# 27 chunks of u turned by VectorE beside the mixer instead of 24, from weight piece 10 on, and spread evenly

## The chip, the cores and the metric

One core of a Trainium2 chip runs the whole kernel. The metric is the time on the device in microseconds, the median over runs. A profile is one execution with the hardware profiler; its span is from the first to the last instruction.

TensorE (PE; its weight loads are PEld), VectorE (DVE), ScalarE (ACT) and GpSimd (POOL) each work through their own instructions in order. SP only issues transfers. Transfers issued by SP, by ScalarE and by POOL go through three queues to the same 16 transfer engines.

## The reference

A decoder layer over 256 tokens of width 1024: a mixer and then a product-key retrieval over 16384 experts (PEER), whose tables `u` and `v` have 16384 rows of 1024 floats each.

```python
h = rmsnorm(x)
proj = h @ w_in                       # 1024 x 6656
... retention, block attention with a relative-position bias, two branches, gates, w_out ...
x = x + merged @ w_out
h2 = rmsnorm(x)
# PEER: 8 heads, the 16 best of 128 x 128 experts for each token
u = u_tab[experts]
a = gelu(einsum('td,thkd->thk', h2, u))
x = x + einsum('thk,thkd->td', gates * a, v_tab[experts])
```

## The kernel before, in words

**The mixer** (to about 250 us) takes all its weights in 72 pieces of 256 rows by 512 columns (512 KB each), in the loop over `i`. SP loads a piece into a ring of six buffers (`raw_ring`, L206). ScalarE cuts off its high half (`rhi`, L151), VectorE the rest (`rlo`, L152), three pieces ahead of TensorE, which multiplies it in 12 matmuls (L234 to L236: high by high, low by high, high by low). Between the pieces `pump` advances the epilogues and the attention a step each. The attention adds the relative-position bias to its scores on VectorE (`pr<-side,bias`, L369), takes the maximum (`smx`, L373), and ScalarE the exponentials (L375). `bias` comes from 8 transfers of 128 KB out of a skewed table, issued by POOL (L840). POOL also has the small powers for the normalisations (`qky`, L158) and the sums of the rotary step (`ra`, L328).

**The dense stage** (about 300 to 635 us) multiplies all of `u`, in 128 chunks of 128 rows, with part of the tokens. A chunk `c` is loaded by SP into the same ring (L674), turned by 8 transposes on TensorE (L732) two chunks ahead, brought back from PSUM by ScalarE, and then multiplied (L1304; 8 products, which the trace counts as 16). In the same time POOL gathers single rows of `u` and `v`, VectorE forms dot products with them, and from about 465 us on one-hot matrices are multiplied in between (L1225, L1226). 14 chunks (`HELD`) are loaded ahead into another buffer and are not in the ring. The third stage (635 to 895 us) does the same with `v`, without transposes.

**The turned chunks** are the subject of the change. `EARLY` lists chunks that are turned during the mixer, one each at the weight pieces in `TURNED`. For the m-th, `early_turns` issues at piece `TURNED[m]` - 4 four transfers of 128 KB on POOL's queue (L742) into a buffer `raw`; at `TURNED[m]` and one piece later VectorE turns half of it each (L746) from `raw` to `dst`; another piece later ScalarE writes `dst` to the tensor `turned` in HBM (L770). In the dense stage SP loads such a chunk from `turned` (L697) and TensorE multiplies it without transposes. There are three buffers for `raw` and three for `dst`: `eraw` and `eT`; `h2` (named `h` in the trace) and a part of `hTf`; and as third first parts of `sa` and `ret`, later the two halves of the attention's tile `pr`.

The order on each engine is the order in which the code is written (`manual_schedule`), so a step that moves in the loop moves on every engine that it uses. Waits are put in where data or buffers need them. Each transfer of POOL's queue gets one of eight semaphores in turn (`DMASW0` to `DMASW7`) and is not issued before the last transfer with the same semaphore has landed.

Of the kernel before, what the change touches and what calls it, by code (L numbers as in the profile page):

```python
# [50 lines left out]
HELD = [0, 1, 2, 8, 14, 21] + list(range(26, 62, 6)) + [61, 66]  # L51
HELD0 = 2
FOLD = 104
TURNED = list(range(14, 36, 2)) + [37, 40, 42, 45, 48, 50, 53, 56, 58, 61, 64, 66, 69]
EARLY_RAW = [0, 1, 2, 0, 1, 2, 0, 1, 2, 0, 1, 0] + [2, 1, 0] * 4
EARLY_AT = [-3 if m == 11 else -4 for m in range(24)]
NPRE = len(TURNED)
EARLY = [3 + 5 * m + (m in (1, 7)) for m in range(NPRE)]
TURN = (124, 126)
TURN0 = 95  # L60
WARM = 8
# [18 lines left out]
def layer_kernel(ctx, tc, x, mix_norm_g, w_in, ret_w_branch, moba_q_gain, moba_k_gain, moba_w_branch,  # L80
# [26 lines left out]
    def raw_tile(n=1):  # L107

        i = raw_count[0] % RAWS
        raw_count[0] += n  # L110
        assert i + n <= RAWS
        return raw_ring[:, i] if n == 1 else raw_ring[:, i:i + n]
# [102 lines left out]
    def products(i):  # L215
# [30 lines left out]
        if k0 + 2 == kc:  # L246
# [11 lines left out]
    early = ([ap.tile([P, D], F32, name="eraw"), h2],  # L258
             [ap.tile([P, D], F32, name="eT"), hTf.rearrange("p k t -> p (k t)")[:, :D]])
# [421 lines left out]
    def load_any(i):  # L681
# [9 lines left out]
        elif i < len(pieces) + NK:  # L691
# [3 lines left out]
            if early_chunk(c):  # L695
                u_raw[c] = raw_tile()
                nc.sync.dma_start(u_raw[c], turned[EARLY.index(c)])  # L697
            else:
# [36 lines left out]
    def early_chunk(c):  # L735
        return c in EARLY

    def load_quarters(queue, dst, c, quarters=range(4)):

        src = peer_u[0, c * P:(c + 1) * P, :].rearrange("(b a) (g d) -> g a b d", a=32, g=4)  # L740
        for g in quarters:
            queue.dma_start(dst[32 * g:32 * g + 32].rearrange("a (b d) -> a b d", b=4), src[g])  # L742

    def turn(dst, src, k):

        V.transpose(dst.rearrange("p (k b a) -> p b k a", k=KC, b=4)[:, :, k],  # L746
                    src.rearrange("p (b k i) -> p b k i", b=4, k=KC)[:, :, k])

    free = []

    def early_buffers(m):

        raw, dst = EARLY_RAW[m], m % 3
        if m >= EARLY_RAW.index(2, 11) and not free:
            t = wk.tile([P, H, S], F32, name="pr").rearrange("p h k -> p (h k)")
            free.extend([t[:, :D], t[:, D:]])
        third = free or [sa[:, KC // 2:].rearrange("p k t -> p (k t)"), ret[:, 1]]
        return (*early[0], third[0])[raw], (*early[1], third[1])[dst]

    def early_turns(i):  # L760

        for m in range(NPRE):
            step = i - TURNED[m]
            if step == EARLY_AT[m]:
                load_quarters(nc.gpsimd, early_buffers(m)[0], EARLY[m])
            if step in (0, 1):
                raw, dst = early_buffers(m)
                turn(dst, raw, slice(4 * step, 4 * step + 4))
            elif step == 2:
                nc.scalar.dma_start(turned[m], early_buffers(m)[1])  # L770
# [30 lines left out]
    for t in range(NT):  # L801
        for q in range(2):
            c = slice(512 * q, 512 * (q + 1))
# [46 lines left out]
    for i in range(n_mixer + 3):  # L850
        load_to(i + 1)
        if i == 8:
            nc.sync.dma_start(decay, c_decay)
        if i == 12:
            nc.sync.dma_start(grow2, row(ffn_norm_g))
        cut(i + 3)
        products(i)
        early_turns(i)
        pump()
# [422 lines left out]
    for c in range(NK):  # L1282
# [11 lines left out]
        m, g = divmod(c - TURN0, 8)  # L1294
# [171 lines left out]
```

## Time and profile before

| | us |
|---|---|
| median of 3 runs (lowest to highest) | 933.49 (931.58 to 933.52) |
| the profiled execution | 930.01 |
| its span | 928.2 |

TensorE's clock was granted in full. Of the page, the first lines give each engine's busy time and share; the slices cut the span into 40 parts of 23.2 us with the busy share of each in tenths; the chain is followed back from the last instruction. In a timeline row stand the start, the length, the engine, line, operation, what it writes and reads, the shape, the count, and in brackets how long the engine stood idle before and what ended that.

### The profile page before, as it was taken

How to read it: one execution, taken by the hardware profiler on the slowest of the kernel's cores; microseconds unless marked ns; L12 is line 12 of the kernel's file. 1: busy time of each engine (PE TensorE's matmuls, PEld its weight loads, DVE VectorE, ACT ScalarE, POOL GpSimd, SP SyncE). 2: the span in 40 equal slices, each digit the busy share in tenths (PEclk: the TensorE clock that was granted, in tenths of full speed). 3: DMA queues.
4: the chain of work that ended last, by engine and by line, in shares of the span. 5: the costliest groups of instructions: out<-in, count | busy, mean ns of one | idle time of the engine just before them, and what ended most of it. 6: DMA issues, size and time to landing. Idle time of an engine off the chain costs nothing.

```text
span 928.2 us, 18735 instructions
## 1 busy us (share of the span) xinstructions
PE 921.4 (99%) x6968; PEld 875.5 (94%) x6968; DVE 801.7 (86%) x1535; ACT 510.2 (55%) x940; POOL 450.4 (49%) x411
## 2 busy tenths in 40 slices
PE   9999999999999999999999999999999999999998
PEld 6887888888999999999999999999999999999997
DVE  6658666888778999999899999886989989898996
ACT  5555655544644535434587777676454545454553
POOL 3547233220102447534557786664656656474530
PEclk9999999999999999999999999999999999999999
DMA  9899998999799999999999999999999999999991
GB/s 312 244 256 296 346 288 259 353 327 292 237 372 383 399 386 351 387 397 378 375 408 405 391 381 369 385 408 373 368 397 408 409 407 409 385 408 379 388 392 59
DMA packets 107018, 328.83 MB, mean 354 GB/s; under 512 B 12237, under 2 KB 16246, under 8 KB 106799
## 3 DMA queue, kind: packets, MB, share of 16 engines
q1 hardware_dynamic: 64092, 183.07, 54.2%
q0 software_dynamic: 37440, 128.52, 38.0%
q10 hardware_dynamic: 5394, 16.05, 4.5%
q8 instruction: 55, 0.90, 0.4%
q14 instruction: 37, 0.30, 0.1%
HBM read 311.78 MB, written 17.33 MB: 355 GB/s over the span
## 4 chain that ended last, share of the span: by engine, by line
PE 73%; DVE 0%; ACT 0%; issue 0%; DVEq 0%
PE acc L1304 25%; PE side L732 10%; PE acc L1336 10%; PE side L1336 9%; PE acc L1337 4%; PE side L1337 4%; PE side L1334 2%; PE acc L1334 2%; PE acc L244 1%; PE acc L243 1%; PE acc L245 1%; PE acc L1226 1%; PE acc L1225 1%; PE side L624 1%; PE side L890 0%; PE side L587 0%
## 5 line engine op out<-in xcount | busy, mean ns | idle before, releaser
L1044 POOL DMA_INDIRECT rows<-in_peer_u_dram,eg x86 | 109.5, 1273 | 77.9 <-DVE rows L1055 37.9
L1044 POOL DMA_INDIRECT rows<-in_peer_v_dram,eg x54 | 100.1, 1854 | 75.4 <-DVE vacc L1132 58.0
L732 PE MATMUL side<-ident,raw_ring 128*128 128x128 f32 x704 | 94.6, 277 | 0.2 <-DMA raw_ring<-in_peer_u_dram 0.2
L732 PEld LDWEIGHTS side<-ident,raw_ring 128*128 128x128 f32 x704 | 85.3, 192 | 0.3 <-issue 0.3
L1270 ACT ACTIVATE cw<-W 128x352 fp32r<-128x352 f32 x58 | 28.9, 498 | 73.7 <-PE acc L1337 73.7
L1175 ACT ACTIVATE oh_buf<-oh_more,tS 128x128 bf16<-128x128 f16 x176 | 58.7, 414 | 12.5 <-DVE oh_more L1170 8.7
L1055 DVE SCALAR_TENSOR_TENSOR rows<-rows,h 128x1024 f32<-128x1024 f32 x43 | 53.5, 1254 | 5.2 <-DMA rows<-in_peer_u_dram,eg 5.2
L1132 DVE SCALAR_TENSOR_TENSOR vacc<-rows,av,vacc 128x1024 f32<-128x1024 f32 x42 | 53.7, 1279 | 0.1
L1304 PE MATMUL acc<-hTd,raw_ring 128*128 128x128 f32 x384 | 46.8, 275 | 0.0
L1271 DVE TENSOR_TENSOR cw<-W,cw 128x352 fp32r<-128x352 f32 x58 | 30.2, 521 | 17.1 <-ACT cw L1270 16.8
L1304 PEld LDWEIGHTS acc<-hTd,raw_ring 128*128 128x128 f32 x384 | 44.8, 192 | 0.0
L1256 POOL TENSOR_TENSOR W<-W,gl 128x256 f32<-128x256 f32 (+19 forms) x31 | 25.6, 825 | 28.3 <-ACT gl L1255 23.4
L1171 DVE TENSOR_TENSOR oh_buf<-oh_more,tM 128x1024 f16<-128x1024 f16 x44 | 32.2, 732 | 2.2
L742 POOL DMA_DIRECT2D eraw<-in_peer_u_dram x36 | 19.8, 555 | 26.5 <-DVE pr L746 14.1
L1170 DVE TENSOR_TENSOR oh_more<-iota,tI 128x1024 f16<-128x1024 f16 x44 | 32.0, 728 | 0.0
L742 POOL DMA_DIRECT2D h<-in_peer_u_dram x32 | 17.4, 551 | 25.2 <-DVE hTf L746 22.6
L1225 PE MATMUL acc<-oh_buf 128*128 128x128 bf16 x176 | 24.4, 219 | 0.0
L1226 PE MATMUL acc<-oh_buf 128*128 128x128 bf16 x176 | 24.4, 219 | 0.0
L1239 ACT ACTIVATE W<-acc 128x512 f32<-128x512 f32 (+20 forms) x44 | 17.0, 387 | 6.6 <-PE acc L1226 4.4
L1258 ACT ACTIVATE W<-acc 128x256 f32<-128x256 f32 (+19 forms) x52 | 18.5, 355 | 3.3 <-PE acc L1304 3.3
L1225 PEld LDWEIGHTS <-oh_buf 128*128 128x128 f16 x176 | 19.8, 113 | 0.0
L1226 PEld LDWEIGHTS <-oh_buf 128*128 128x128 f16 x176 | 19.7, 114 | 0.0
(2685 smaller groups left out, 3412.9 us busy)
## 6 DMA issues: line engine op xcount, KB each, us to landing
raw_ring<-in_peer_v_dram SPq DMA_DIRECT2D x100, 512.0 KB
raw_ring<-in_peer_u_dram SPq DMA_DIRECT2D x88, 512.0 KB
raw_ring<-in_w_in_dram SPq DMA_DIRECT2D x52, 512.0 KB
W<-in_peer_v_dram SPq DMA_DIRECT2D x28, 512.0 KB
raw_ring<-turned SPq DMA_DIRECT2D x24, 512.0 KB
raw_ring<-in_peer_w_q_dram SPq DMA_DIRECT2D x16, 512.0 KB
W<-in_peer_u_dram SPq DMA_DIRECT2D x14, 512.0 KB
eraw<-in_peer_u_dram POOLq DMA_DIRECT2D x36, 128.0 KB
```

The lines of the kernel that those rows point to most:

```text
L732: T.transpose(p[:, k * P:(k + 1) * P], r.rearrange("p (i k) -> p k i", k=KC)[:, 4 * q + k], ident)
L742: queue.dma_start(dst[32 * g:32 * g + 32].rearrange("a (b d) -> a b d", b=4), src[g])
L1044: G.indirect_dma_start(out=r, out_offset=None, in_=tab, in_offset=bass.IndirectOffsetOnAxis(ap=eg[:, j:j + 1], axis=0))
L1055: V.scalar_tensor_tensor(r, r, 1.0, h, op0=OP.mult, op1=OP.mult, accum_out=av[:, j:j + 1])
L1132: V.scalar_tensor_tensor(a, r, av[:, j:j + 1], a, op0=OP.mult, op1=OP.add)
L1175: A.activation(o1[:, j], hot[:, 0, :, j], AF.Copy, scale=tS[:, t, k + j:k + j + 1])
L1225: T.matmul(p[:, j * P:(j + 1) * P], hi, o1, start=True, stop=False)
L1226: T.matmul(p[:, j * P:(j + 1) * P], lo, o1, start=False, stop=True)
L1304: T.matmul(pa[:, n:n + NA], uT[:, k * P:(k + 1) * P], hT[:, k], start=(c % 2 == 0 and k == 0), stop=(k == KC - 1), skip_group_check=True)
L1334: T.matmul(o[b][:, :ND], vh[:, n], w, start=False, stop=False, skip_group_check=True)
L1336: T.matmul(o[b][:, :2 * ND], vh[:, n], w, start=(c == 0), stop=False, skip_group_check=True)
L1337: T.matmul(o[b][:, :ND], vl[:, n], w[:, :ND], start=False, stop=(c == NK - 1), skip_group_check=True)
```

## The change

`TURNED` gets three more places: pieces 10 and 12 at the front, and one more between 37 and 70, where the distance is 2.5 pieces throughout. `EARLY`, which was every fifth chunk from 3 to 118, is now spread evenly over the chunks 3 to 120 that are not held: 3, 7, 12, 17, 22, 27, 31, 37, 42, 47, 52, 57, 62, 67, 71, 75, 79, 83, 87, 91, 96, 100, 104, 108, 112, 116, 120. The tables for the `raw` buffer and the time of the load are gone: every load is issued four pieces ahead, `raw` and `dst` both go by m modulo 3, and the halves of `pr` come in at m = 14 (piece 40).

```diff
-TURNED = list(range(14, 36, 2)) + [37, 40, 42, 45, 48, 50, 53, 56, 58, 61, 64, 66, 69]
-EARLY_RAW = [0, 1, 2, 0, 1, 2, 0, 1, 2, 0, 1, 0] + [2, 1, 0] * 4
-EARLY_AT = [-3 if m == 11 else -4 for m in range(24)]
+TURNED = list(range(10, 36, 2)) + [37, 40, 42, 45, 47, 50, 52, 55, 57, 60, 62, 65, 67, 70]
 NPRE = len(TURNED)
-EARLY = [3 + 5 * m + (m in (1, 7)) for m in range(NPRE)]
+LEAD = 4
+LATE = 14
+EARLY = [c for c in range(3, 121) if c not in HELD]
+EARLY = [EARLY[round(m * (len(EARLY) - 1) / (NPRE - 1))] for m in range(NPRE)]
...
-        raw, dst = EARLY_RAW[m], m % 3
-        if m >= EARLY_RAW.index(2, 11) and not free:
+        if m == LATE and not free:
...
-        return (*early[0], third[0])[raw], (*early[1], third[1])[dst]
+        return [(*early[i], third[i])[m % 3] for i in range(2)]
...
-            if step == EARLY_AT[m]:
+            if step == -LEAD:
```

Line numbers up to the turned chunks are one higher in the changed kernel. POOL's instructions from the skewed table on, before:

```order
L832 DMA skew<-rr 8x16x384
L158 TENSOR_TENSOR qky<-qkss,minus_half 128x16 x2
L840 DMA bias<-skew 16x8x256 x8
L742 DMA eraw<-in_peer_u_dram 32x4x256 x4
L742 DMA h_75<-in_peer_u_dram 32x4x256 x4
L742 DMA sa<-in_peer_u_dram 32x4x256 x4
L328 TENSOR_TENSOR ra<-ra,rb__621 128x512
```

And now:

```order
L832 DMA skew<-rr 8x16x384
L159 TENSOR_TENSOR qky<-qkss,minus_half 128x16
L743 DMA eraw<-in_peer_u_dram 32x4x256 x4
L159 TENSOR_TENSOR qky<-qkss,minus_half 128x16
L743 DMA h_75<-in_peer_u_dram 32x4x256 x4
L840 DMA bias<-skew 16x8x256 x8
L743 DMA sa<-in_peer_u_dram 32x4x256 x4
L743 DMA eraw<-in_peer_u_dram 32x4x256 x4
L743 DMA h_75<-in_peer_u_dram 32x4x256 x4
L329 TENSOR_TENSOR ra<-ra,rb__635 128x512
```

The four loads of the first new chunk stand ahead of the second `qky`, and those of the second new chunk ahead of the eight transfers of `bias`. With the waits, the transfers of `bias` in the changed kernel are these:

```order
L743 DMA h_75<-in_peer_u_dram 32x4x256 [waits DMASW5_49]
L840 DMA bias<-skew 16x8x256 [waits DMASW6_49]
L840 DMA bias<-skew 16x8x256 [waits DMASW7_49]
L840 DMA bias<-skew 16x8x256 [waits DMASW0_49]
L840 DMA bias<-skew 16x8x256 [waits DMASW1_49]
L840 DMA bias<-skew 16x8x256 [waits DMASW2_49]
L840 DMA bias<-skew 16x8x256 [waits DMASW3_49]
L840 DMA bias<-skew 16x8x256 [waits DMASW4_49]
L840 DMA bias<-skew 16x8x256 [waits DMASW5_49]
```

Semaphores 6, 7, 0 and 1 were last given to the four loads of the first new chunk, 2 to 5 to those of the second. VectorE about pieces 14 to 17 of the weights (`rlo__493`, 532, 556 and 579), before:

```order
L152 TENSOR_TENSOR rlo__493<-raw_ring,rhi__492 128x1024
L369 TENSOR_TENSOR pr<-side,bias 128x4x128
L152 TENSOR_TENSOR rlo__532<-raw_ring,rhi__531 128x1024
L369 TENSOR_TENSOR pr<-side,bias 128x4x128
L152 TENSOR_TENSOR rlo__556<-raw_ring,rhi__555 128x1024
L373 TENSOR_REDUCE smx<-pr 128x8
L152 TENSOR_TENSOR rlo__579<-raw_ring,rhi__578 128x1024
```

And now (the same pieces are `rlo__502`, 542, 568 and 592):

```order
L747 STREAM_TRANSPOSE eT<-eraw 128x4x4x32
L153 TENSOR_TENSOR rlo__502<-raw_ring,rhi__501 128x1024
L747 STREAM_TRANSPOSE eT<-eraw 128x4x4x32
L370 TENSOR_TENSOR pr<-side,bias 128x4x128
L153 TENSOR_TENSOR rlo__542<-raw_ring,rhi__541 128x1024
L747 STREAM_TRANSPOSE hTf<-h_75 128x4x4x32
L370 TENSOR_TENSOR pr<-side,bias 128x4x128
L153 TENSOR_TENSOR rlo__568<-raw_ring,rhi__567 128x1024
L747 STREAM_TRANSPOSE hTf<-h_75 128x4x4x32
L374 TENSOR_REDUCE smx<-pr 128x8
L153 TENSOR_TENSOR rlo__592<-raw_ring,rhi__591 128x1024
```

Two transposes of the first new chunk stand ahead of `pr<-side,bias`, and the two of the second between it and `smx`. SP's loads in the last part of the dense stage, before:

```order
L697 DMA raw_ring<-turned 128x1024
L674 DMA raw_ring<-in_peer_u_dram 128x1024 x4
L697 DMA raw_ring<-turned 128x1024
L674 DMA raw_ring<-in_peer_u_dram 128x1024 x4
L697 DMA raw_ring<-turned 128x1024
```

And now:

```order
L698 DMA raw_ring<-turned 128x1024
L675 DMA raw_ring<-in_peer_u_dram 128x1024 x3
L698 DMA raw_ring<-turned 128x1024
L675 DMA raw_ring<-in_peer_u_dram 128x1024 x3
L698 DMA raw_ring<-turned 128x1024
```

From chunk 67 on three chunks, mostly, stand between two turned ones, where there were four.

## The prediction

> **What bounds the kernel now.** I read the engine line and the slices of the page first, then the chain of waits, then stretches of the timeline.
>
> ```profile
> PE 921.4 (99%) x6968; PEld 875.5 (94%) x6968; DVE 801.7 (86%) x1535; ACT 510.2 (55%) x940; POOL 450.4 (49%) x411
> PE   9999999999999999999999999999999999999998
> DMA  9899998999799999999999999999999999999991
> PE 73%; DVE 0%; ACT 0%; issue 0%; DVEq 0%
> ```
>
> TensorE is busy in every slice and the chain is TensorE's own work, so a microsecond taken off TensorE is a microsecond gained as long as nothing makes it wait, and one that it stands still is lost for good. But the transfer engines are as full as TensorE, so the margins by which data arrives ahead of it are the second thing to read.
>
> The gain lies in the stage over the 128 chunks of u. The chain of waits there, in order of time (start, duration, what):
>
> ```profile
> 483.40 0.95 PE side L732 x8
> 484.34 1.79 PE acc L1304 x16
> 486.58 0.95 PE side L732 x8
> 487.52 1.79 PE acc L1304 x16
> 489.31 0.89 PE side L732 x8
> 490.20 1.79 PE acc L1304 x16
> 492.43 1.84 PE acc L1304 x16
> 494.72 0.95 PE side L732 x8
> ```
>
> Each chunk has 8 transposes (L732) and its products (L1304); at 492.43 a turned chunk has products alone. From one chunk's transposes to the next takes 486.58 - 483.40 = 3.18 us, the turned one 494.72 - 492.43 = 2.29 us: 0.89 us less.
>
> The price lies in the mixer, where the early loads and the 8 transfers of `bias` share POOL's one queue. POOL's timeline there:
>
> ```profile
> 24.61 3.98 POOL L158 TENSOR_TENSOR qky<-qkss,minus_half 128x16 f32<-128x16 f32 x1 [3.05 <-DVE gain L834]
> 36.03 2.92 POOL L158 TENSOR_TENSOR qky<-qkss,minus_half 128x16 f32<-128x16 f32 x1 [7.44 <-DVE qkss L298]
> 38.90 4.27 POOL L840 DMA_DIRECT2D bias<-skew  x8
> 45.62 2.43 POOL L742 DMA_DIRECT2D eraw<-in_peer_u_dram  x4 [2.45 <-DMA bias<-skew]
> 52.31 0.55 POOL L742 DMA_DIRECT2D h<-in_peer_u_dram  x1 [0.46 <-DMA bias<-skew]
> 53.76 0.55 POOL L742 DMA_DIRECT2D sa<-in_peer_u_dram  x1 [0.90 <-DMA eraw<-in_peer_u_dram]
> 57.86 0.55 POOL L742 DMA_DIRECT2D sa<-in_peer_u_dram  x1 [0.60 <-DMA eraw<-in_peer_u_dram]
> ```
>
> A transfer on this queue waits until the one eight before it has landed (the order of the program shows it as one of eight semaphores). So these rows date landings: the first `bias` transfer is in by 45.62, the eighth by 52.31, the ninth (first of `eraw`) by 53.76 and the twelfth (last of `eraw`) by 57.86. Twelve transfers of 128 KB issued from 38.90 on take until 57.86, eight until 52.31.
>
> VectorE, in order, waits for all eight of `bias` before its next operation:
>
> ```profile
> 45.12 1.23 DVE L152 TENSOR_TENSOR rlo__493<-raw_ring,rhi__492 128x1024 fp32r<-128x1024 f32 x1 [2.50 <-ACT rhi__492 L151]
> 52.76 0.69 DVE L369 TENSOR_TENSOR pr<-side,bias 128x512 f32<-128x512 f32 x1 [6.41 <-DMA eraw<-in_peer_u_dram]
> 53.37 1.22 DVE L152 TENSOR_TENSOR rlo__532<-raw_ring,rhi__531 128x1024 fp32r<-128x1024 f32 x1
> 56.23 1.21 DVE L373 TENSOR_REDUCE smx<-pr 128x8 f32<-128x1024 f32 x1
> 60.12 1.23 DVE L152 TENSOR_TENSOR rlo__579<-raw_ring,rhi__578 128x1024 fp32r<-128x1024 f32 x1 [2.67 <-ACT rhi__578 L151]
> 65.01 0.70 DVE L746 STREAM_TRANSPOSE eT<-eraw 128x512 f32<-128x512 f32 x1
> 65.64 0.66 DVE L324 TENSOR_TENSOR ra<-acc,rope 128x512 f32<-128x512 f32 x1
> 66.98 1.17 DVE L152 TENSOR_TENSOR rlo__639<-raw_ring,rhi__638 128x1024 fp32r<-128x1024 f32 x1
> ```
>
> The wait of 6.41 us at 52.76 is put down to `eraw`, but L369 reads `bias`, and it ends 0.45 us after the eighth `bias` transfer is known to be in. Queued behind it are the low halves of the weights that TensorE multiplies (L152). When TensorE takes them:
>
> ```profile
> 56.17 0.39 PE L235 MATMUL acc<-rlo__532,hh 128*128 128x512 f32 x1
> 62.50 0.40 PE L235 MATMUL acc<-rlo__579,hh 128*128 128x512 f32 x1
> 68.39 0.40 PE L235 MATMUL acc<-rlo__639,hh 128*128 128x512 f32 x1
> ```
>
> Piece 15 (rlo__532) is ready at 53.37 + 1.22 = 54.59, 1.58 us ahead; piece 17 (rlo__579) at 61.35, 1.15 us ahead; piece 19 (rlo__639) at 68.15, 0.24 us ahead. These are the thinnest margins of the mixer after its first pieces, and they stand just where the two new chunks are put.
>
> **The change, part by part.**
>
> Three chunks fewer to transpose: 3 x 0.89 = -2.67 us (with 0.95 of the L732 rows instead, -2.85). ScalarE's 6 evacuations go too; ScalarE is 55% busy and is worth nothing here. All three lie late: 14 turned chunks up to chunk 68 before and after, 10 beyond it before, 13 now.
>
> The transfers of that stage. A turned chunk is read once like any other, so the bytes stay; they are asked for in less time. The rows of the stages and the one wait of TensorE in it:
>
> ```profile
> 450.00:550.00 100.00, 100.00 (x982) 100.00 (x981) 95.85 (x170) 76.51 (x218) 70.46 (x60) 1.00 1.02 398
> 550.00:600.00 50.00, 49.83 (x496) 49.67 (x494) 46.48 (x78) 37.56 (x109) 34.95 (x30) 1.00 1.03 375
> 600.00:635.00 35.00, 35.00 (x341) 35.00 (x340) 25.49 (x42) 23.80 (x61) 20.89 (x20) 1.00 1.03 404
> 596.28 1.14 PE L732 MATMUL side<-ident,raw_ring 128*128 128x128 f32 x8 [0.17 <-DMA raw_ring<-in_peer_u_dram]
> ```
>
> The columns after the length are busy PE, PEld, DVE, ACT and POOL, the clock, the share of the transfer engines and GB/s. At 596 TensorE already waits for a load, so around 570 to 605 (chunks 105 to 118) the margin is gone. Between chunks 95 and 118 one more chunk is turned than before (6 against 5), so TensorE asks 0.89 us sooner there and can wait up to that much. Between 0 and 0.89 I take +0.4, the middle. VectorE at 96% in 450:550 would be at 97% with 1% less time: no wait. [...]
>
> The two new early loads. Chunk 0's four transfers now follow the first `qky` (end 24.61 + 3.98 = 28.59), and POOL stands idle until 36.03, so they and VectorE's two transposes of 0.63 us (65.64 - 65.01) are hidden by VectorE's and POOL's own waits (VectorE stands 2.50 us before 45.12). Chunk 1's four come after the second `qky`, at 38.95, where `bias` stood, and `bias` follows them. `bias` then is the fifth to twelfth transfer of the burst, not the first to eighth. The twelfth landed by 57.86 and the eighth by 52.31: +5.55 us. The semaphore of the one eight before does not starve the queue: the last four of `bias` go out when chunk 1's have landed, as `eraw` did at 45.62.
>
> Two things move this. How the queues share the engines in that time (queue, packets, MB, share), first from 52.3 to 57.9, and then the write of one turned chunk, from 66 to 70:
>
> ```profile
> q0 software_dynamic: 321, 0.91, 72.1%
> q1 hardware_dynamic: 221, 0.42, 32.2%
> ...
> q10 hardware_dynamic: 144, 0.52, 32.4%
> ```
>
> With VectorE standing still SP runs out of free ring buffers, so less weight traffic (q1) competes: without any, 5.55 x 0.721 = 4.0 us is the lower bound. Against it, ScalarE now writes chunk 0 out at about 48 us, 0.52 MB that takes 32.4% of 4 us = 1.3 us: 6.85 us is the upper bound. They pull opposite ways and I stay at 5.55, the measured row. [...]
>
> What follows on VectorE: between L369 and the low half of piece 17 stand two more transposes (chunk 1's), 1.26 us, which lengthen the way L369, smx, ScalarE's exponentials, piece 17. So L152 of piece 15 comes 5.55 later (margin 1.58: TensorE waits 3.97), piece 17 comes 6.81 later (1.15: 5.66 in all) and piece 19 also 6.81 later (0.24): 6.57 us in all. Behind 70 us the chunks stand at the distances that they had, TensorE is as late as everything else, and the margins are as before: +6.57. Bounds: 4.0 + 1.02 = 5.0 and 6.85 + 1.02 = 7.9.
>
> The third new chunk stands at piece 70; its last transpose (0.63 us) falls before the last residual's chain. Between 0 and +0.63; before it VectorE idles about as long there, so 0. The buffers of the other chunks change places without a transfer being later than four pieces ahead: 0.
>
> **Sum.** +6.57 - 2.67 + 0.4 = +4.3 us on the profiled execution's 930.01 us. That one stands 3.5 us under the median of the runs, 933.49; the forecast is on the median: 937.8 us. What a measurement tells from no change is about 0.2%, 1.9 us.
>
> **Rivals.**
> 1. The queue moves faster than the rows say, and `bias` comes 0 to 3 us late: stall up to 4.1, net between -1.9 and +1.9, say 934.5. For it: the twelve would move with VectorE and SP silent. Against: even without all of q1 the rows give 4.0.
> 2. The end on the other side: `bias` is not held up. If the four of chunk 1 cost the queue under about 1.2 us, the stall (d + 1.02) is less than the 2.27 gained in the dense stage. Place: POOL's queue at 39 to 52 us; it decides at `bias` in by 53.5. With no delay at all but the two transposes, 1.26 - 0.24 = 1.0 is lost at piece 19, net -1.3; if that is hidden too -2.3: about 931.5. For it: the engines' queues run in parallel. Against: the ninth to twelfth landed one after another, 53.76 to 57.86.
> 3. The transfers of the dense stage eat the whole gain: +6.57 - 2.67 + 2.67 gives 940.1. For it: the wait at 596.28; against: 398 to 404 GB/s on both sides of it.
>
> **Chances.** The forecast with its own bounds, +2.2 (5.0 - 2.85) to +6.1 (7.9 - 2.67 + 0.89), 0.66; rival 3 and worse, 0.11; rival 1, 0.13; rival 2, 0.10. So slower 0.77, same 0.13, faster 0.10. Range: the forecast's own is 935.7 to 939.6; with rival 3 and half of rival 1 it is 934.0 to 941.0.
>
> **What would show it.** Right: `bias` issued from about 41 us on; L370 (`pr`) starting at 57 to 60 after an idle time of 10 us or more on VectorE; TensorE idle 3 to 5 us at about 56 and again at about 66; the mixer's end some 6 us later; in the dense stage 24 transposes fewer and the stage 2 to 3 us shorter. Wrong: L370 by 54 us, or a pause in TensorE's products that another engine makes up later, or a dense stage no shorter.

## The result, and the profile after

| | before | after |
|---|---|---|
| median of 5 runs each, taken together (lowest to highest), us | 933.23 (930.88 to 933.52) | 939.20 (937.92 to 940.66) |
| ratio, 95% interval | 1 | 1.0071 (1.0054 to 1.0089) |
| profiled execution, its span, us | 930.01, 928.2 | 938.77, 937.0 |

The change costs 0.71%, which is 5.0 to 8.3 us by the interval. Four lines of its page: busy time by engine, the slices of TensorE and of the transfer engines, and the chain of waits by engine.

```profile
PE 922.7 (98%) x6944; PEld 874.4 (93%) x6944; DVE 806.8 (86%) x1541; ACT 507.1 (54%) x934; POOL 454.7 (49%) x423
PE   8989999999999999999999999999999999999998
DMA  9999998999899999999999999999999999999991
PE 60%; DVE 23%; DMA 10%; POOL 2%; issue 2%; ACT 1%; SPq 0%; ACTq 0%; DVEq 0%; POOLq 0%
```

TensorE has 24 matmuls fewer and is busy 1.3 us longer; the third slice (47 to 70 us) is no longer full. The chain that was TensorE's alone now runs over VectorE for 23% and over transfers for 10%.

Where the 8.75 us of span are. POOL's timeline in the mixer after the change:

```profile
29.30 2.26 POOL L743 DMA_DIRECT2D eraw<-in_peer_u_dram  x4
36.78 2.93 POOL L159 TENSOR_TENSOR qky<-qkss,minus_half 128x16 f32<-128x16 f32 x1 [5.22 <-DVE qkss L299]
39.68 2.23 POOL L743 DMA_DIRECT2D h<-in_peer_u_dram  x4
41.90 2.11 POOL L840 DMA_DIRECT2D bias<-skew  x4
44.48 2.17 POOL L840 DMA_DIRECT2D bias<-skew  x4 [0.46 <-DMA h<-in_peer_u_dram]
...
58.80 0.55 POOL L743 DMA_DIRECT2D eraw<-in_peer_u_dram  x1 [0.45 <-DMA bias<-skew]
```

Chunk 1's loads (`h`) stand before `bias`. The issue at 58.80 waits for the eighth `bias` transfer (8 later on the queue), which therefore is in only then; before, it was at 52.31. VectorE's timeline, which waits for it:

```profile
45.87 1.23 DVE L153 TENSOR_TENSOR rlo__502<-raw_ring,rhi__501 128x1024 fp32r<-128x1024 f32 x1 [1.88 <-ACT rhi__501 L152]
...
58.83 0.69 DVE L370 TENSOR_TENSOR pr<-side,bias 128x512 f32<-128x512 f32 x1 [11.12 <-DMA sa<-in_peer_u_dram]
59.44 1.22 DVE L153 TENSOR_TENSOR rlo__542<-raw_ring,rhi__541 128x1024 fp32r<-128x1024 f32 x1
60.57 0.70 DVE L747 STREAM_TRANSPOSE hTf<-h 128x512 f32<-128x512 f32 x1
...
67.38 1.23 DVE L153 TENSOR_TENSOR rlo__592<-raw_ring,rhi__591 128x1024 fp32r<-128x1024 f32 x1 [2.67 <-ACT rhi__591 L152]
...
74.24 1.17 DVE L153 TENSOR_TENSOR rlo__653<-raw_ring,rhi__652 128x1024 fp32r<-128x1024 f32 x1
```

This execution was 0.75 us later than the one before from its start on (45.87 against 45.12). Apart from that, L370 starts 58.83 - 52.76 - 0.75 = 5.32 us later, and the low half of piece 19 (`rlo__653`, before 66.98) 6.51 us later. The stage borders of the kernel before, from TensorE's timeline (first product of chunk 0, first of the third stage):

```profile
299.05 1.17 PE L1304 MATMUL acc<-hTf,rhi__2891 128*128 128x128 f32 x9
638.69 0.41 PE L1336 MATMUL side<-cw,rhi__7232 128*128 128x352 f32 x1
```

And of the kernel after:

```profile
306.24 0.94 PE L1304 MATMUL acc<-hTf,rhi__2912 128*128 128x128 f32 x7
647.39 0.41 PE L1336 MATMUL side<-cw,rhi__7214 128*128 128x352 f32 x1
```

The dense stage begins 7.19 us later (0.75 of the start and 6.44 of stall) and takes 341.15 us instead of 339.64, although 24 transposes are gone; the third stage takes as long as before. TensorE's waits in it after the change (in total, times, longest):

```profile
PE acc L1225 <- DVE oh_buf L1171: 1.8, 2, 1.1
PE side L733 <- DMA raw_ring<-in_peer_u_dram: 0.5, 1, 0.5
PE acc L1304 <- ACT W L1258: 0.3, 1, 0.3
```

And the three windows that the prediction read:

```profile
450.00:550.00 100.00, 99.72 (x967) 99.41 (x967) 97.14 (x176) 72.89 (x205) 66.36 (x57) 1.00 1.01 398
550.00:600.00 50.00, 48.38 (x478) 47.79 (x477) 47.26 (x78) 34.11 (x103) 33.53 (x30) 1.00 1.02 374
600.00:635.00 35.00, 34.19 (x335) 33.69 (x334) 30.34 (x47) 26.22 (x69) 22.78 (x20) 1.00 1.03 402
```

Before there was one wait, of 0.17 us. VectorE is at 97% in the first window, as forecast, and yet TensorE now waits for one-hots (L1171) that VectorE makes. With every start of a TensorE step added up that comes over 0.1 us later than its kind usually does, the waits come to about 4.3 us against 0.3 before, which is more than the 2.67 us of the three chunks. The chain of waits back from one of them shows what held it (start, length, what):

```profile
597.51 13.68 DMA rows<-in_peer_u_dram,eg
...
611.22 1.23 DVE rows L1055 x2
612.45 0.62 DVE oh_more L1170
...
613.16 0.70 DVE oh_buf L1171
613.86 0.05 issue
613.91 0.25 PE acc L1225
```

The one-hot stands on VectorE behind a dot product (L1055) whose gathered row took 13.68 us to land.

### The profile page after: what moved, and what is told of

Read it like the earlier page. It is cut to its first block, busy times and chain, and to the rows that moved or that the text cites. A ratio compares the mean times of both kernels' runs of the same rounds, so it can differ in the third digit from the quotient of the medians.

```text
span 937.0 us, 18689 instructions
## 1 busy us (share of the span) xinstructions
PE 922.7 (98%) x6944; PEld 874.4 (93%) x6944; DVE 806.8 (86%) x1541; ACT 507.1 (54%) x934; POOL 454.7 (49%) x423
## 4 chain that ended last, share of the span: by engine, by line
PE 60%; DVE 23%; DMA 10%; POOL 2%; issue 2%; ACT 1%; SPq 0%; ACTq 0%; DVEq 0%; POOLq 0%
PE acc L1336 9%; PE side L1336 9%; DVE rows L1055 7%; PE acc L235 6%; PE acc L236 6%; PE acc L237 6%; DMA rows<-in_peer_u_dram,eg 5%; PE acc L1337 4%; PE side L1337 4%; PE acc L1304 2%; DVE oh_more L1170 2%; DVE oh_buf L1171 2%; PE side L1334 2%; PE acc L1334 2%; PE acc L245 1%
## 5 line engine op out<-in xcount | busy, mean ns | idle before, releaser
L733 PE MATMUL side<-ident,raw_ring 128*128 128x128 f32 x680 | 91.3, 277 | 0.5 <-DMA raw_ring<-in_peer_u_dram 0.5
L733 PEld LDWEIGHTS side<-ident,raw_ring 128*128 128x128 f32 x680 | 82.4, 192 | 0.7 <-issue 0.6
L1055 DVE SCALAR_TENSOR_TENSOR rows<-rows,h 128x1024 f32<-128x1024 f32 x43 | 53.1, 1239 | 7.3 <-DMA rows<-in_peer_u_dram,eg 7.2
L1304 PE MATMUL acc<-hTd,raw_ring 128*128 128x128 f32 x432 | 52.8, 275 | 0.3 <-ACT W L1258 0.3
L1304 PEld LDWEIGHTS acc<-hTd,raw_ring 128*128 128x128 f32 x432 | 50.4, 192 | 0.5 <-ACT W L1258 0.5
L1271 DVE TENSOR_TENSOR cw<-W,cw 128x352 fp32r<-128x352 f32 x58 | 30.2, 521 | 18.7 <-ACT cw L1270 18.3
L1171 DVE TENSOR_TENSOR oh_buf<-oh_more,tM 128x1024 f16<-128x1024 f16 x44 | 33.2, 754 | 2.2
L743 POOL DMA_DIRECT2D h<-in_peer_u_dram x36 | 19.7, 554 | 28.7 <-DVE hTf L747 18.8
L974 POOL DMA_DIRECT2D eg<-ei x4 | 2.3, 567 | 37.0 <-issue 34.4
```

Source lines behind the costliest of these rows:

```text
L733: T.transpose(p[:, k * P:(k + 1) * P], r.rearrange("p (i k) -> p k i", k=KC)[:, 4 * q + k], ident)
L1055: V.scalar_tensor_tensor(r, r, 1.0, h, op0=OP.mult, op1=OP.mult, accum_out=av[:, j:j + 1])
L1171: V.tensor_tensor(o2, hot[:, 1:2].to_broadcast(shape), tM[:, t, :, None, k:k + 4].to_broadcast(shape), op=OP.mult)
L1304: T.matmul(pa[:, n:n + NA], uT[:, k * P:(k + 1) * P], hT[:, k], start=(c % 2 == 0 and k == 0), stop=(k == KC - 1), skip_group_check=True)
```

## The experiments

"Dense begins" and "dense takes" are those two borders in each run's one profile; the ratio is that of the timed runs to the kernel before. Line numbers differ by one to three where an edit adds lines. Kernels with the mixer of before begin the dense stage between 299.05 and 301.08 us, so less than 2 us in that column means nothing. Where the dense stage has its 24 chunks (before, mixer alone, before with half dots) it takes 339.64 to 340.24 us, so differences below 0.6 us in the next column mean nothing either.

| run | dense begins | dense takes | ratio (95%) |
|---|---|---|---|
| before | 299.05 | 339.64 | 1 |
| after | 306.24 | 341.15 | 1.0071 (1.0054 to 1.0089) |
| bias ahead of chunk 1's loads | 304.96 | 340.78 | 1.0041 (1.0027 to 1.0056) |
| mixer alone | 305.16 | 340.07 | 1.0065 (1.0043 to 1.0088) |
| dense alone | 299.67 | 341.07 | 1.0010 (0.9999 to 1.0022) |
| dense, extras early | 300.93 | 340.15 | 1.0025 (1.0006 to 1.0043) |
| dense, extras late | 301.08 | 339.66 | 1.0004 (0.9985 to 1.0024) |
| chunk 1's loads at piece 6 | 303.33 | 341.74 | 1.0031 (1.0014 to 1.0049) |
| no chunk at piece 12 | 299.15 | 339.67 | 1.0004 (0.9989 to 1.0019) |
| dense alone, half dots | 299.87 | 339.81 | 0.9978 (0.9958 to 0.9998) |
| before, half dots | 299.39 | 340.24 | 0.9981 (0.9962 to 1.0000) |
| dense alone, half rows | 300.51 | 377.50 | 1.0437 (1.0403 to 1.0472) |
| before, half rows | 300.46 | 390.36 | 1.0455 (1.0434 to 1.0477) |
| dense alone, half loads | 300.05 | 338.04 | 0.9957 (0.9941 to 0.9973) |

**Mixer alone.** The kernel after, with three of its turned chunks unused:

```diff
+EARLY = [4, 5] + [3 + 5 * m + (m in (1, 7)) for m in range(24)] + [6]
+USED = EARLY[2:26]
-        return c in EARLY
+        return c in USED
```

> The mixer of the changed kernel (27 chunks loaded, turned and written at the same pieces), but the dense stage uses only 24 of them, the 24 of the kernel before; the three others (the first, the second and the last turned) are written out and never read. Theory (two separate effects): the mixer ends 6.4 to 6.6 us later than before, the dense stage takes 339.6 us as before, total about 939.7 against 933.2. Rival (the dense stage's new waits come from the mixer's delay or from the other order of buffers, not from the 27 chunks): the dense stage takes 341 to 343 us here too and the total is 941 or more.

It lost 0.65% (6.1 us of 932.5), nearly all of the change's cost, and its dense stage took 340.07 us with a single wait, 0.6 us for a load. So the mixer's stall is an effect of its own.

**Dense alone.** The kernel before, with the chunks that count as turned replaced:

```diff
+USED = [3, 7, 12, 17, 22, 27, 31, ..., 104, 108, 112, 116, 120]
-        return c in EARLY
+        return c in USED
-                nc.sync.dma_start(u_raw[c], turned[EARLY.index(c)])
+                nc.sync.dma_start(u_raw[c], turned[USED.index(c) % NPRE])
```

> The kernel before with its mixer untouched (24 chunks turned), and the dense stage of the changed kernel: 27 chunks at the changed kernel's places are read as turned ones; the last three of them read a slot that holds another chunk, so their numbers are another chunk's. Theory (VectorE with the gathered rows is the second limit of the dense stage, so it takes no shorter time): dense stage 340.5 to 341.5 us, total 934 to 935.5, +1 to +2 on the kernel before, with waits on L1170 (one-hots) near chunks 105 to 118. Rival (the dense stage loses its gain only because it starts late in the changed kernel): dense stage 337 to 337.5, total about 931.

The stage took 341.07 us, the ratio is 1.0010: no gain, with no stall ahead of it (the total, 933.11 us, is 0.9 below the theory's range). A gain of 2.67 us would be 0.9971, which lies outside the interval. The waits are those of the kernel after:

```profile
PE acc L1226 <- DVE oh_buf L1172: 1.2, 1, 1.2
PE acc L1305 <- ACT W L1259: 0.7, 1, 0.7
PE side L733 <- DMA raw_ring<-in_peer_u_dram: 0.2, 1, 0.2
```

**Extras early, extras late.** The same edit with the 24 chunks of before and three more: 6, 16, 25 in one run, 116, 120, 122 in the other.

> The kernel before with its mixer untouched, and 27 chunks read as turned in the dense stage: the 24 of the kernel before at their places and three more (6, 16, 25) in its first fifth, where no one-hots are built; the three read slots of other chunks. Theory (VectorE is the limit over the whole second half, so time won ahead of it is given back there): dense stage 339 to 341 us, total 933 to 935. Rival (it is the denser places of turned chunks between 95 and 118 that lose, by their transfers): dense stage near 337, total about 930.7.

> The mixer of before, and 27 chunks read as turned: the 24 of before and three more at 116, 120 and 122, behind the last one-hots, where VectorE is 73% busy (25.49 of 35 us) and the transfers are as full as everywhere; the three read slots of other chunks. Theory (VectorE's list is the limit up to the last one-hots only): the whole 2.67 us is gained, dense stage 336.9 to 337.5, total about 930.5. Rival (the transfers are the limit): the loads of these chunks come late instead, dense stage 338.5 to 340, total 932 to 934.

Neither gained: ratios 1.0025 and 1.0004. None of the three placements gained; what moves is the place of the loss. In the early run nearly all is lost in one wait at 455, for ScalarE, which stood itself; in the late one at 630, again behind ScalarE. TensorE's timeline in the early run:

```profile
455.39 0.82 PE L1305 MATMUL acc<-hTf,rhi__4769 128*128 128x128 f32 x5 [2.80 <-ACT W L1259]
```

ScalarE's in the early run:

```profile
452.36 0.31 ACT L1002 ACTIVATE gates<-gates 128x128 f32<-128x128 f32 x1 [4.87 <-DVE gates L987]
```

ScalarE's in the late run:

```profile
630.10 0.26 ACT L1119 ACTIVATE av<-av 128x64 f32<-128x64 f32 x1 [6.67 <-DVE rows L1056]
```

Both times ScalarE waits in order for the end of a list on VectorE (the exponentials of the gates, the Gelu of all dot products), and the evacuations that TensorE needs stand behind it. My theory for the late run, that VectorE limits only up to the last one-hots, fell: the dot products there wait for gathered rows.

**Half dots.** VectorE's dot products over half of the columns, in the dense-alone kernel and in the kernel before:

```diff
-        V.scalar_tensor_tensor(r, r, 1.0, h, ..., accum_out=av[:, j:j + 1])
+        V.scalar_tensor_tensor(r[:, :D // 2], r[:, :D // 2], 1.0, h[:, :D // 2], ..., accum_out=av[:, j:j + 1])
```

> The kernel of the run on the dense stage alone (mixer of before, 27 chunks read as turned at the changed kernel's places), and VectorE's dot products with the gathered rows of u (L1055, 1.22 us each) taken over half of the columns, so that each takes some 0.65 us; the rows are gathered whole as before, so the transfers stay. The dots leave out half of each sum. Theory (VectorE's list of work is the second limit, and TensorE's gain is given back where it waits for what VectorE makes): VectorE falls from 97% to some 85% busy in 450 to 550 us, the waits on L1171 and L1258 go, and the dense stage takes 336.9 to 337.5 us instead of 341.1: total 929 to 930.5. Rival (the transfers are the second limit, and VectorE is late only because its rows are): the dense stage still takes over 339.5 us and the total is over 932.

> The control for it: the kernel before with the same halved dot products. Theory: nothing waits for VectorE in the dense stage of before (its waits have one row, for a load), so the stage stays at 339.3 to 339.7 us and the total within 0.2% of before. Rival (VectorE already costs the kernel before something that the waits do not show): the stage falls below 339.

VectorE fell to 73% in 450 to 550 us and the waits near 453 and 475 us went. Those from 575 to 610 stayed: the theory that VectorE's work is the only second limit fell too. VectorE's timeline in the dense-alone run with half dots:

```profile
604.04 0.69 DVE L1056 SCALAR_TENSOR_TENSOR rows<-rows,h 128x512 f32<-128x512 f32 x1 [1.73 <-DMA rows<-in_peer_u_dram,eg]
604.65 0.69 DVE L1171 TENSOR_TENSOR oh_more<-iota,tI 128x1024 f16<-128x1024 f16 x1
605.45 0.69 DVE L1172 TENSOR_TENSOR oh_buf<-oh_more,tM 128x1024 f16<-128x1024 f16 x1
```

TensorE's waits in the same run:

```profile
PE acc L1226 <- DVE oh_buf L1172: 1.2, 1, 1.2
PE side L733 <- DMA raw_ring<-in_peer_u_dram: 1.0, 1, 1.0
```

A lighter VectorE only waits longer for its rows (1.73 us before 604.04) and the one-hot behind them is as late. The control shows that lighter dots are worth as much with 24 chunks (0.9981); against it the 27 chunks bring nothing (0.9978). The control's dense stage, 340.24 us, missed its range (339.3 to 339.7) upwards, so its one profile does not show where the timed runs gained.

**Half loads.** Dense alone with whole dots, and 45 of the untouched chunks loaded over half of their columns:

```diff
-                u_raw[c] = load_rows(peer_u, c)
+                u_raw[c] = raw_tile()
+                n = D // 2 if 60 <= c <= 121 else D
+                nc.sync.dma_start(u_raw[c][:, :n], peer_u[0, c * P:(c + 1) * P, :n])
```

> The run on the dense stage alone (mixer of before, 27 chunks read as turned, VectorE's dots whole again), and 45 of the untouched chunks between 60 and 121 are loaded over half of their columns only (256 KB instead of 512, in packets of 2 KB over the same 128 rows); the other half keeps what lay in the buffer. VectorE's work and every instruction's place stay. Theory (two limits: VectorE's work makes the waits near 453 and 475 us, the transfers those from 575 to 610): the first stay, about 1.2 us, the second, 2.9 us, go; the dense stage takes 337.8 to 338.4 us instead of 341.1, the total falls some 3 us below that run's 933.1. Rival (VectorE's own work is late there too): the waits on L1171 at 590 to 606 us stay and the stage is over 340.

The stage took 338.04 us, where the theory had 337.8 to 338.4, and the ratio fell to 0.9957. TensorE's only wait in the stage:

```profile
PE acc L1307 <- ACT W L1261: 1.1, 1, 1.1
```

Two windows of the same run:

```profile
450.00:550.00 100.00, 98.88 (x966) 98.56 (x965) 97.37 (x176) 73.60 (x212) 70.67 (x58) 1.00 0.93 337
550.00:600.00 50.00, 50.00 (x500) 50.00 (x499) 48.91 (x83) 38.36 (x110) 36.52 (x32) 1.00 0.99 340
```

VectorE is as full as ever (48.91 of 50). The transfer engines move less (337 and 340 GB/s, where the kernel after has 398 and 374); their busy share falls to 0.93 in the first window and only to 0.99 in the second. TensorE waits for nothing after 456 us, and VectorE's waits for gathered rows between 545 and 640 us fall from 5.1 us (dense alone) to 0.6. So the late waits are the transfers', and the early one comes through VectorE: each goes with its own relief and stays with the other's. (What makes VectorE late there is a gathered row that lands at about 380 us, ahead of the loads halved here; it is shown in the next section.) The kernel before was not run with half loads; its one wait in this stage is of 0.17 us.

**Half rows.** An earlier attempt at the same, with gathers of 64 rows instead of 128 and half dots:

```diff
+        n = 64 if j < NU and j not in gs["got"] else P
-        G.indirect_dma_start(out=r, ..., in_offset=bass.IndirectOffsetOnAxis(ap=eg[:, j:j + 1], axis=0))
+        G.indirect_dma_start(out=r[:n], ..., in_offset=bass.IndirectOffsetOnAxis(ap=eg[:n, j:j + 1], axis=0))
```

> The dense stage with 27 turned chunks behind the mixer of before, VectorE's dots halved as in the earlier run, and now each gather of a row of u fetches 64 of its 128 rows (256 KB instead of 512), so that the transfer engines have room as well; the rest of those dot products is left out. Theory (the transfers hold the late rows, the late one-hots and the late loads between 575 and 610 us): the dense stage takes 336.8 to 337.4 us, its waits on L1171 and on raw_ring are gone, total about 927.5, which is 2.3 to 2.8 us below the same kernel with 24 chunks. Rival (something that is neither VectorE's work nor the bytes, such as the order of the instructions on the queues, gives the gain back): the dense stage stays at 339 us or more and level with the 24 chunks.

> The control: the kernel before with the same halved dots and the same halved gathers of u. Theory: the dense stage takes 339.2 to 339.6 us, total about 930. Rival (the order of the queues): the same as the run with 27 chunks.

Both missed. Fewer bytes made the stage 38 and 50 us longer than with half dots alone: the transfer engines moved 254 GB/s at a share of 0.97, as the window of the dense-alone run with half rows shows:

```profile
300.00:637.00 337.00, 308.66 (x2795) 305.27 (x2794) 233.91 (x809) 176.69 (x447) 143.71 (x157) 0.98 0.97 254
```

The same window with half dots alone, 387 GB/s:

```profile
300.00:637.00 337.00, 334.77 (x3151) 334.05 (x3150) 251.93 (x845) 203.69 (x514) 172.94 (x180) 1.00 1.01 387
```

These two decide nothing on the question.

**Bias first.** The kernel after, with the loop of empty steps ahead of the `bias` transfers one shorter, so that they stand ahead of chunk 1's loads:

```diff
-        for _ in range(5):
+        for _ in range(4):
             yield
```

> The changed kernel with one step moved: the 8 transfers of bias are issued one piece earlier, so that on POOL's queue they stand ahead of chunk 1's four loads instead of behind them. Everything else (27 turned chunks, the same transposes and writes in the mixer) stays. Theory (the mixer's stall is the place of bias in the queue): L370 starts near 53.5 us instead of 58.83; what remains of the stall is chunk 1's two transposes ahead of piece 17's low half, 1.0 to 1.5 us; the dense stage (first product of chunk 0 to first product of the third stage) stays at about 341 us; total about 936, +2.5 to +3.5 on the kernel before. Rival (the stall is the price of turning two more chunks there, whatever the order): L370 still after 57 us, total 939 to 940.

L370 went back to 52.93 us, and yet the stall hardly shrank: the dense stage begins 5.7 us late instead of 6.4 (without this execution's later start, 0.22). VectorE's timeline:

```profile
52.93 0.69 DVE L370 TENSOR_TENSOR pr<-side,bias 128x512 f32<-128x512 f32 x1 [5.74 <-DMA h<-in_peer_u_dram]
59.30 0.71 DVE L747 STREAM_TRANSPOSE hTf<-h 128x512 f32<-128x512 f32 x1 [4.55 <-DMA h<-in_peer_u_dram]
```

Now chunk 1's own transpose waits, 4.55 us, for the loads that went behind. My theory had overlooked that: the two sets have 12 transfers together, VectorE needs all of them by 59 us, and their order mostly says for which it waits. The time, 936.59 us, came out where the theory had it (about 936) with 5.7 us of stall where it had 1.0 to 1.5; that is luck. What the timed runs gained over the kernel after beyond those 0.7 us is not explained by this profile.

**Loads early.** The kernel after, with chunk 1's loads in POOL's idle time behind chunk 0's:

```diff
-            if step == -LEAD:
+            if step == -(LEAD + 2 * (m == 1)):
```

> The changed kernel with chunk 1's four loads issued two pieces earlier, at piece 6, right behind chunk 0's and ahead of the second qky on POOL; bias keeps its place behind that qky. Theory (the twelve transfers that POOL's queue has to carry between 39 and 58 us are the stall, whatever their order; moved into POOL's idle time at 31 to 36 us they are hidden): L370 starts at 53 to 55 us and chunk 1's transposes wait for nothing, the stall falls from 6.45 to 1 to 3 us, and the total is 934 to 936. Rival (the stall comes from the transposes and writes of the two chunks themselves): L370 near 58 us again, or the wait elsewhere, total 938 to 940.

L370 started at 55.24 and chunk 1's transposes waited for nothing:

```profile
55.24 0.69 DVE L370 TENSOR_TENSOR pr<-side,bias 128x512 f32<-128x512 f32 x1 [8.01 <-DMA bias<-skew]
```

TensorE reached piece 20 at 76.52 (before 72.93), that is 3.3 us late without this execution's later start (0.25): 2.2 of the queue and 1.0 of the two transposes, as their sum says. The dense stage began 4.0 us late; where the other 0.7 us were lost is not shown. Both L370 and the stall missed the theory's ranges (53 to 55, 1 to 3) by a little. In time, 1.0031 instead of 1.0071.

**No piece 12.** 26 chunks, without the one at piece 12:

```diff
-TURNED = list(range(10, 36, 2)) + ...
+TURNED = [10] + list(range(14, 36, 2)) + ...
-LATE = 14
+LATE = 13
```

> The changed kernel without the chunk at piece 12: 26 chunks, the new ones at pieces 10 and 70, EARLY spread evenly over 26. Theory (the stall is the price of chunk 1 alone, by its four transfers on POOL's queue and its two transposes; chunk 0's are hidden in POOL's idle time, the last one's too): L370 near 53 us, the mixer ends within 1 us of before, the dense stage gains little or nothing (339 to 340.5), total 932 to 934.5, within 0.2% of before. Rival (chunk 0's loads, at 29 us, or its write at 48 us delay bias as well): the mixer still ends 3 us later and the total is 935 to 937.

With the indices shifted by one, the chunk at piece 34 is turned in parts of `sa` and `ret` that the mixer has begun to fill, so this run's numbers are not the layer's; its times can be read. L370 started at 52.96, the dense stage began at 299.15, the ratio is 1.0004. All of this is in the theory's ranges: without chunk 1 the stall is gone, though the first and the last new chunk are still there. No version that computes the layer beat the kernel before, and none is proposed.

## Why the prediction was right or wrong

The time came out 1.4 us above the forecast, and the sign was right. That the number is so near is partly luck: rival 3, with the gain of the dense stage eaten, had 940.1, which is 0.9 us off, so the time alone cannot choose between the two. Between the two profiled executions the change is 8.76 us where the forecast had 4.3; between the medians it is 5.97, and the interval of the timed runs, 5.0 to 8.3, holds the profile's stall and stage together (6.44 + 1.51 = 7.95). The profile also shows one of the prediction's own signs of being wrong, a dense stage no shorter.

- **Bias on POOL's queue, +5.55: right**, 5.32 measured. The lower end of 4.0 needed the weight queue to fall silent, and it did not: q1 had 30.2% of the transfer engines from 52.3 to 58.8 us, and q10, which writes chunk 0, had 23.0%. So 4.0, which the prediction worked out from POOL's share of 72.1%, is an estimate that this trace does not test.
- **Two more transposes, stall +6.57 in all: right in size**, 6.44 measured. Not as described: the forecast had TensorE wait at 56 and again near 66. It waits once, and then runs slowly. TensorE's timeline after the change:

```profile
60.71 0.77 PE L236 MATMUL acc<-rlo__542,hh 128*128 128x512 f32 x1 [3.63 <-DVE rlo__542 L153]
61.28 0.63 PE L237 MATMUL acc<-rhi__541,hl 128*128 128x512 f32 x1
```

One microsecond behind it in the windows (the clock is the third figure from the end):

```profile
61.00:62.00 1.00, 1.00 (x3) 0.81 (x3) 1.00 (x3) 0.00 (x0) 0.00 (x0) 0.50 0.66 145
```

After 3.63 us of waiting the granted clock is 0.50 from 61 to 64 us, and matmuls take 0.63 us instead of 0.39. That costs about 1.7 us (eight products take 3.53 us, from 60.71 to 64.24, which at 0.227 each take 1.81; 0.227 is the step at a granted clock of 1.00, nine products in 2.04 us from 54.65 to 56.69), but VectorE's list sets when piece 19 is ready, and it was late by 6.51 us anyhow, so the slow clock filled time in which TensorE would have waited. The forecast's sum held because it followed the data and not the clock.
- **First and third new chunk hidden, 0: right**, by the run without piece 12, whose dense stage begins at 299.15 (before 299.05).
- **Three transposed chunks fewer, -2.67, and a loss of +0.4 to the transfers: wrong in the second term.** The loss was 4.2 us (341.15 - 339.64 + 2.67). The step that failed bounded it by what one more turned chunk between 95 and 118 could ask too early, 0.89. All three count wherever they stand (extras early: no gain). There TensorE and ScalarE come 2.66 us earlier to the exponentials of the gates (ScalarE's step ahead of that wait, the table load, starts 145.28 us into the stage, before 147.94), VectorE's list comes 0.53 us later, and nearly the whole gain is lost in that one wait. The other failed sentence is "97%: no wait". VectorE makes things that TensorE and ScalarE need at fixed places of their order, and with 96 to 97% of its time taken it does not catch up what it loses. In the kernel after it loses the wait for a late row. ScalarE's wait ahead of the same exponentials, before:

```profile
449.95 0.31 ACT L1001 ACTIVATE gates<-gates 128x128 f32<-128x128 f32 x1 [1.68 <-DVE gates L986]
```

And after:

```profile
458.77 0.31 ACT L1001 ACTIVATE gates<-gates 128x128 f32<-128x128 f32 x1 [3.31 <-DVE gates L986]
```

Here ScalarE comes no earlier (its table load starts at 446.99 before and at 454.18 after, both 147.94 us into the stage); VectorE comes 1.63 us later. It lost that time 74 us ahead, at one dot product. VectorE there, before:

```profile
376.17 1.22 DVE L1055 SCALAR_TENSOR_TENSOR rows<-rows,h 128x1024 f32<-128x1024 f32 x1
```

And after:

```profile
385.00 1.23 DVE L1055 SCALAR_TENSOR_TENSOR rows<-rows,h 128x1024 f32<-128x1024 f32 x1 [1.51 <-DMA rows<-in_peer_u_dram,eg]
```

From 385.00 on every dot product starts 1.63 us later in the stage than before, up to the gates. The row was late because POOL issued its gather 2.4 us later, behind two small transfers that waited on the queue for earlier gathers (0.92 us and, in this line, 1.48):

```profile
375.55 0.53 POOL L1018 DMA_DIRECT2D gx<-gates  x1 [1.48 <-DMA rows<-in_peer_u_dram,eg]
```

The five runs with whole dots and all 27 chunks at the changed kernel's places wait at this dot product (1.19 to 2.34 us); before, mixer alone, the two with extras elsewhere and the one without piece 12 do not (extras early waits 0.69 us at the next one). Why the earlier gathers land later there is open.

- **How full the transfers were.** With gathered rows of 4 KB among the traffic of the kernel after the engines are at a share of 1.02 to 1.03 at 374 to 402 GB/s between 550 and 635 us, and data is late: TensorE waits 0.5 us for a load in the stage, and VectorE 5.7 us for gathered rows between 552 and 648 us. At 340 GB/s (half loads, 550 to 600 us, a share of 0.99) TensorE waits for nothing.
- **Rivals.** The dense stage went the way of the third (the whole gain eaten, and 1.5 us more in this profile), the mixer that of the forecast; rival 2 needed `bias` not to be held up, and even with chunk 1's loads moved ahead 2.2 us remained.

Open: why the dense stage of some profiles takes longer than before, by up to 2.1 us (chunk 1's loads at piece 6), that is, lost more than its gain. Of the timed runs of the three placements two (1.0010 and 1.0004) cannot tell that from nothing. The third, extras early (1.0025), can; ten of its twelve timed runs had a mean granted clock of 0.995 to 0.998, where all of dense alone had 0.999 or 1.0, so a part of its loss may be the clock's. That is not shown.

## What to carry to other kernels

In this stage TensorE, VectorE and the transfers were full together (99.7%, 97% and a share of 1.01 from 450 to 550 us), and time taken off TensorE was given back at the next place where it met the others: 2.67 us taken off, 4.2 lost in the kernel after, and no gain at any of the three placements (1.0010, 1.0025, 1.0004). So before crediting a gain, ask which of the streams that it waits for also becomes shorter, and reckon with losing the whole of it, not one thin margin. VectorE, with 73.17 of 74 us taken from 385 to 459 us, passed a single late row on: 1.63 us, 74 us further. The twelve transfers on POOL's queue that VectorE needed by 59 us cost their sum (the four more held `bias` up by 5.32 us), and reordering them mostly changed the name of the wait (5.7 us of stall instead of 6.4). Ahead of a change to such a queue, look for an idle stretch of it: moving chunk 1's loads there took the queue's part of the stall from 5.32 to 2.2 us.

## What was unexpected of the hardware

TensorE's clock: 3.63 us of waiting were followed by a granted clock of 0.50 for some 3 us, in which the products of 512 columns came every 427 ns (six from 61.28 to 63.84 us) instead of every 227. But a wait of 2.50 us was followed by it as well (bias first, clock 0.50 from 62 to 65 us), and one of 2.80 us was not (extras early, 1.00 throughout at 452 to 460 us). The mean granted clock was 0.996 to 0.998 in all five timed runs of the kernel after and 0.997 or 0.998 in all six of mixer alone (3.3 us of waiting in its profile), but only in five of the twelve of bias first. So in these runs the length of the wait alone does not tell whether the clock falls.

With gathers of 64 rows instead of 128 all 16 transfer engines together moved 254 GB/s instead of 387, at almost the same busy share (0.97 and 1.01). SP's packets slowed down too: from 300 to 400 us one took 214 ns instead of 147 (worked out from its queue's share of the 16 engines' time and its packets). No run here shows why.
